# A fused attention and linear-attention block on one core: GpSimd's arithmetic moved to VectorE, and the gates' reciprocals rebuilt from log, exp and a Newton step

## The chip, the cores and the metric

The kernel runs on one core of a Trainium2 chip. The metric is the device time of one execution in microseconds: 2037.1 us, the median of three runs (2032.62 to 2038.48). The profile shows one more execution, which took 2037.28 us.

## The reference

One layer over 1024 tokens of width 2048, all in float32. A vector of shift, scale and gate is computed from `c` by a 2048 x 6144 product; the normalised input is modulated by it and projected by `w_in` (2048 x 7184). Group A has eight heads of differential attention, group B four heads of gated linear attention with a state carried from chunk to chunk of 64 tokens. Both outputs are normalised per head and multiplied by the SiLU of a projected gate. An output projection, a gated residual and a last RMSNorm end it. What matters here, in short:

```
proj = hn @ w_in                       # dq dk dv dg | gq gk gv gg glr
p    = softmax(mask(q k^T * scale))    # two maps per head
a    = p[:, 0] - lam * p[:, 1]
A    = rmsnorm(a @ v) * (1 - lam_init) * silu(dg)
B    = rmsnorm(gla(gq, gk, gv, log_sigmoid(glr @ w2 + b) / 16)) * silu(gg)
out  = rmsnorm(x + gate * (concat(A, B) @ w_out))
```

## The kernel before

Each matrix is held as two parts, a high one rounded to the type in which TensorE multiplies (fp32r) and a low one, the rest. A product takes three matmuls: high by high, high by low, low by high. So every weight piece goes through a small pipeline in `wload` (L169 to L186): SyncE loads 128 x 1024 numbers (512 KB) from memory into `wr` (two buffers), ScalarE casts them into the high half of `w` (L180, three buffers), and GpSimd subtracts that from the original into the low half (L181). TensorE then uses the piece in 24 matmuls of 512 columns, or 48 of 256. There are 298 pieces. For the 32 of the first stage the caller names VectorE in GpSimd's place (`first_a`, `first_b`).

The stages, in order of time: 0 to 200 us computes scale and shift from `wada` and accumulates the first projections beside it; then come eight units (two halves of 512 tokens by four groups), each with two attention heads (`attention`), projections and one linear-attention head (`gla`); from about 1600 us the output projection (L928 on). In attention, VectorE takes the row maxima from PSUM (L609), ScalarE the exponentials (L618), VectorE scales the second map by a column (L632) and adds the scaled first (L633), TensorE transposes, ScalarE and VectorE split the result (`split`, L229), and TensorE multiplies by the values (L660 to L662).

Beside the weights GpSimd does the second product of the rotary embedding (L520), three products of each head's normalisation (L566, L578, L580, but for the last head), and half of the 16 low parts of the second half's input (L906). It issues no DMA.

`silu_gate` (L238 to L245) makes a gate: ScalarE's exp(-x), one added on VectorE (L242), VectorE's reciprocal in two pieces of 256 columns (L244), and one product with the gate and a weight column (L245). There are 32 such gates of 128 x 512.

Two side jobs are fed through a staging tile of two buffers (`run_ahead`, L828): the second half's input is normalised row by row, and the residual gate is computed from `wgate`, four blocks of 16 rows, each row added on VectorE to `gacc` (L859). Their loads (L834) stand in the same SyncE queue as the weights' (L178).

The order on each engine is fixed when the program is built: the Tile framework simulates a timeline, takes priorities given in the code (weights are put 300 ahead, WSPAN), and writes one queue for each engine. An engine does its queue in that order; an instruction whose inputs are not there holds all behind it.

Of the kernel before, what the change touches and what calls it, by code (L numbers as in the profile page):

```python
# [10 lines left out]
F32 = mybir.dt.float32  # L11
F32R = mybir.dt.float32r
BF16 = mybir.dt.bfloat16
AF = mybir.ActivationFunctionType
# [5 lines left out]
P = 128  # L20
# [16 lines left out]
EVAC = 0  # L37
WSPAN = 300
FIN = 3
RCP = 256  # L40
PE_P = (4, 9, 14)
DVE0 = (1, 3, 5, 7, 9, 12)
DVE1 = (1, 3, 5, 7, 8, 9, 10, 12, 13, 14)
# [53 lines left out]
def body(ctx, tc, A, out):  # L97
# [71 lines left out]
    def wload(src, n, lo_eng=None, span=WSPAN, tile_=None):  # L169
        w_n[0] += 1  # L170
        with tc.high_priority(offset=span):
            raw = wr_p.tile([P, 1024], F32, name=f"wr{w_n[0]}", tag="wr")
            dst = raw[:, :n]
            if len(src.shape) == 3:
                dst = dst.rearrange("p (a b) -> p a b", a=src.shape[1])
            elif len(src.shape) == 4:
                dst = dst.rearrange("p (a b c) -> p a b c", a=src.shape[1], b=src.shape[2])
            nc.sync.dma_start(dst, src)  # L178
            w = tile_ if tile_ is not None else w_p.tile([P, 2, 1024], F32R, name=f"w{w_n[0]}", tag="w")
            paced = SC.copy(w[:, 0, :n], raw[:, :n])  # L180
            (lo_eng or G).tensor_tensor(w[:, 1, :n], raw[:, :n], w[:, 0, :n].bitcast(F32), ALU.subtract)  # L181
        for _ in range(pops(w_n[0])):
            if later:
                with tc.issue_after(paced.ins):
                    later.pop(0)()
        return w  # L186
# [42 lines left out]
    def split(hi, lo, src, lo_eng=None):  # L229
        SC.copy(hi, src)  # L230
        (lo_eng or V).tensor_tensor(lo, src, hi.bitcast(F32), ALU.subtract)  # L231
# [3 lines left out]
        nc.sync.dma_start(t, A["rope"][:, :, half * TOK:(half + 1) * TOK])  # L235
        return t

    def silu_gate(dst, src, wcol, tmp):  # L238
        SC.activation(tmp, src, AF.Exp, scale=-1.0)
        if dst is not src:  # L240
            SC.copy(dst, src)
        V.tensor_scalar_add(tmp, tmp, 1.0)  # L242
        for i in range(0, TOK, RCP):
            V.reciprocal(tmp[:, i:i + RCP], tmp[:, i:i + RCP])  # L244
        V.scalar_tensor_tensor(dst, dst, wcol, tmp, ALU.mult, ALU.mult)  # L245


    st_ctx = ExitStack()
# [231 lines left out]
    nc.sync.dma_start(ind, A["ind"])  # L480
    nc.sync.dma_start(dnw, A["dnw"])
    nc.sync.dma_start(gnw, A["gnw"])
    V.tensor_scalar_mul(dnw, dnw, 1.0 - LAM_INIT)
    ltri_f = misc.tile([P, 2, TOK], F32, name="ltri_f", tag="rt", bufs=2)
    nc.sync.dma_start(ltri_f[:, 0, :P], A["ltri"])
    V.tensor_copy(ltri, ltri_f[:, 0, :P])
# [25 lines left out]
    def rope(src, nm):  # L512
        rt = misc.tile([P, 2, TOK], F32, name=f"rt_{nm}", tag="rt", bufs=2)
        t1, sw = rt[:, 0, :], rt[:, 1, :]
        for m_ in range(2):
            for hh in range(2):
                o, i_ = m_ * 64 + hh * 32, m_ * 64 + (1 - hh) * 32
                SC.copy(sw[o:o + 32, :], src[i_:i_ + 32, :])  # L518
        V.tensor_mul(t1, src, rope_t[:, 0, :])
        G.tensor_tensor(sw, sw, rope_t[:, 1, :], ALU.mult)  # L520
        V.tensor_add(t1, t1, sw)
        return t1

# [59 lines left out]
    def attention(half, h, qt, kb, vb, g_t):  # L583
# [8 lines left out]
        for grp in range(2):  # L592
            at = []
            for b in (2 * grp, 2 * grp + 1):
# [34 lines left out]
                a_ = []  # L629
                for pi, (kk, n) in enumerate(pieces):  # L630
                    p0, p1 = pt[0, pi][:, :n], pt[1, pi][:, :n]
                    V.tensor_scalar(p1, p1, sm[:, 12:13], None, ALU.mult)  # L632
                    V.scalar_tensor_tensor(p0, p0, sm[:, 10:11], p1, ALU.mult, ALU.add)  # L633
                    a_.append(pt[0, pi])
                at.append(a_)
# [25 lines left out]
                    PE.matmul(dst, vh, aT[:, 1, sl], start=False, stop=False, skip_group_check=True)  # L661
                    PE.matmul(dst, vl, aT[:, 0, sl], start=False, stop=last and k == 1, skip_group_check=True)  # L662
            SC.copy(y[:, grp * 256:(grp + 1) * 256], av[:, :256])
        wf, wr2 = norm_stats([y], f"d{half}{h}", P, eps_l, V if (half, h) == (1, HEADS - 1) else G)
        V.scalar_tensor_tensor(g_t, wf[:, 0, :], sq_max, g_t, ALU.is_lt, ALU.mult)
        r_ = norm_finish(wf, eps_l, V if (half, h) == (1, HEADS - 1) else G)
        V.tensor_mul(y, y, r_)
        V.tensor_mul(y, y, g_t)
        mix_out(y, wr2, half, h)
# [90 lines left out]
    def unit(half, g, first, kdec):  # L760
# [4 lines left out]
        def gate_tile(i):  # L765
            s_ = src("dg", i)
            g_t = s_ if first else acc_p.tile([P, TOK], F32, name=f"g{half}_{i}", tag="g", bufs=2)
            tmp = misc.tile([P, 2, TOK], F32, name=f"gt{half}_{i}", tag="rt", bufs=2)
            silu_gate(g_t, s_, dnw, tmp[:, 0, :])
            return g_t  # L770

        def make_gq():
# [33 lines left out]
        for j in range(2):  # L806
            s_ = src("gg", 2 * g + j)
            tmp = misc.tile([P, 2, TOK], F32, name=f"ggt{half}{g}{j}", tag="rt", bufs=2)
            silu_gate(gg[:, j, :], s_, gnw[:, j:j + 1], tmp[:, 0, :])
        swap = half == 0 and g == GHEADS - 1  # L810
        if not first:
            pss = proj_a(A["wina"][A_AT[("gv", g)]], hn)
# [83 lines left out]
    def second_hn():  # L896
        while later:
            later.pop(0)()
        for k0 in range(0, KT, 2):
            tag = ("ka", "va", "kb")[k0 // 2 % 3]  # L900
            r3 = hd_p.tile([P, 2, TOK], F32, name=f"xtb{k0}", tag=tag, bufs=2 if tag == "kb" else None)
            nc.sync.dma_start(r3, hn_d[k0 // 2])
            for kk in range(2):
                kt = k0 + kk
                hn[kt] = hn_p.tile([P, 2, TOK], F32R, name=f"hn{kt}", tag=f"hn{kt}")
                split(hn[kt][:, 0, :], hn[kt][:, 1, :], r3[:, kk, :], lo_eng=V if kk else G)  # L906


    later += run_ahead(norm_rows())
# [137 lines left out]
```

## Time and profile before

| | |
|---|---|
| median of three runs | 2037.1 us |
| profiled execution | 2037.28 us, of which the span of instructions 2035.5 us |
| mean granted TensorE clock | 0.979 of full speed |
| TensorE matmuls busy | 1934.8 us, 95% |
| VectorE busy | 1364.1 us, 67% |
| ScalarE busy | 880.2 us, 43% |
| GpSimd busy | 762.8 us, 37% |

An engine is busy while an instruction of its own runs, also when this instruction stands still inside and waits for something that the profile does not show. The time outside the span (1.8 us) is not touched by the change. PEclk is the granted share of TensorE's clock in a stretch; 1.00 is 2.4 GHz, 0.5 is 1.2 GHz.

### The profile page before, as it was taken

What the parts mean: (1) busy time and instruction counts of PE and PEld (TensorE: products, weight loads), DVE (VectorE), ACT (ScalarE), POOL (GpSimd) and SP (SyncE); (2) the same over time, 40 slices, a digit from 0 to 9 for tenths busy, and PEclk for the clock granted to TensorE, in tenths of its full rate; (3) what the DMA queues carried; (4) which work ended last, traced back from release to release, by engine and by line L of the source; (5) the groups of instructions that cost most, each with busy time, mean ns of one, the idle gap of its engine ahead of it and who ended that gap; (6) DMA issues with size and microseconds to landing.
All of it is one profiled execution on the core that took longest, in us unless ns stands there. A gap on an engine that the chain in (4) does not pass through costs nothing.

```text
span 2035.5 us, 29315 instructions
## 1 busy us (share of the span) xinstructions
PE 1934.8 (95%) x11238; PEld 1695.4 (83%) x11238; DVE 1364.1 (67%) x2305; ACT 880.2 (43%) x1686; POOL 762.8 (37%) x357
## 2 busy tenths in 40 slices
PE   7999899999888999999998999899988999899998
PEld 5888888898778888889898888888876898688888
DVE  7998775577798658746675686667786664622234
ACT  4212655455433555544435544354444443422223
POOL 0000544424433446643443334353343334244442
PEclk9999999999999999999999999999998999899999
DMA  9874434332654343433343323433243642557443
GB/s 366 296 263 130 144 107 146 117 98 85 206 188 145 116 146 114 141 103 97 95 150 109 103 87 105 154 96 104 84 156 101 220 137 89 177 201 253 160 145 124
DMA packets 112192, 298.19 MB, mean 146 GB/s; under 512 B 11146, under 2 KB 32138, under 8 KB 111540
## 3 DMA queue, kind: packets, MB, share of 16 engines
q1 hardware_dynamic: 112052, 296.32, 44.2%
q8 instruction: 88, 1.44, 0.3%
q14 instruction: 52, 0.43, 0.1%
HBM read 258.00 MB, written 38.28 MB: 146 GB/s over the span
## 4 chain that ended last, share of the span: by engine, by line
PE 62%; DVE 20%; issue 6%; DMA 6%; ACT 4%; POOL 2%; SPq 0%; DVEq 0%; POOLq 0%; ACTq 0%
PE pa L219 5%; PE pa L220 5%; PE pa L221 5%; PE pa L990 4%; PE pa L991 4%; PE pa L992 4%; DMA stage<-in_wgate 2%; DVE gacc L859 2%; PE pb_dk L191 2%; PE pb_dk L193 2%; PE pb_dk L192 2%; PE pb_gg L191 2%; PE pb_gg L193 2%; PE pb_gg L192 2%; DVE p L632 1%
## 5 line engine op out<-in xcount | busy, mean ns | idle before, releaser
L181 POOL TENSOR_TENSOR w<-wr,w 128x1024 fp32r<-128x1024 f32 (+2 forms) x265 | 643.2, 2428 | 951.5 <-ACT w L180 883.6
L180 ACT CAST w<-wr 128x1024 fp32r<-128x1024 f32 (+2 forms) x297 | 304.3, 1025 | 439.1 <-PE pa L992 86.2
L219 PE MATMUL pa<-w,hn 128*128 128x256 f32 (+1 forms) x1152 | 330.9, 288 | 5.9 <-DVE gq L776 1.8
L221 PE MATMUL pa<-w,hn 128*128 128x256 f32 (+1 forms) x1152 | 332.0, 288 | 0.0
L220 PE MATMUL pa<-w,hn 128*128 128x256 f32 (+1 forms) x1152 | 331.8, 288 | 0.0
L219 PEld LDWEIGHTS pa<-w,hn 128*128 128x128 f32 x1152 | 223.6, 194 | 8.9 <-DVE gq L776 2.1
L221 PEld LDWEIGHTS pa<-w,hn 128*128 128x128 f32 x1152 | 223.8, 194 | 2.1 <-issue 0.7
L220 PEld LDWEIGHTS pa<-w,hn 128*128 128x128 f32 x1152 | 224.0, 194 | 1.8 <-issue 0.2
L618 ACT ACTIVATE p<-s,sm 128x512 f32<-128x512 f32 (+2 forms) x192 | 111.2, 583 | 207.3 <-DVE sm L615 113.5
L990 PE MATMUL pa<-w,mx 128*128 128x512 f32 x384 | 150.4, 393 | 0.3 <-DVE h L935 0.3
L991 PE MATMUL pa<-w,mx 128*128 128x512 f32 x384 | 150.4, 392 | 0.0
L992 PE MATMUL pa<-w,mx 128*128 128x512 f32 x384 | 149.7, 392 | 0.0
L609 DVE TENSOR_REDUCE sm<-s 128x1 f32<-128x512 f32 (+2 forms) x192 | 105.3, 550 | 49.8 <-PE s L606 47.4
L935 DVE TENSOR_TENSOR h<-pa,gbs 128x512 f32<-128x512 f32 (+1 forms) x24 | 14.9, 639 | 134.3 <-PE pa L992 120.6
L520 POOL TENSOR_TENSOR rt_k<-rt_k,rope 128x512 f32<-128x512 f32 x16 | 23.2, 1451 | 205.2 <-ACT rt_k L518 204.5
L231 DVE TENSOR_TENSOR aT<-tp,aT 128x512 fp32r<-128x512 f32 (+1 forms) x80 | 50.1, 626 | 72.4 <-ACT aT L230 72.3
L191 PE MATMUL pb_dg<-hn,w 128*128 128x512 f32 x224 | 89.2, 398 | 0.0
L193 PE MATMUL pb_dg<-hn,w 128*128 128x512 f32 x224 | 88.9, 397 | 0.0
L191 PE MATMUL pb_dk<-hn,w 128*128 128x512 f32 x224 | 88.9, 397 | 0.0
L192 PE MATMUL pb_dg<-hn,w 128*128 128x512 f32 x224 | 88.8, 396 | 0.0
L191 PE MATMUL pb_gg<-hn,w 128*128 128x512 f32 x224 | 88.7, 396 | 0.0
L193 PE MATMUL pb_dk<-hn,w 128*128 128x512 f32 x224 | 88.6, 395 | 0.0
(362 smaller groups left out, 4999.8 us busy)
## 6 DMA issues: line engine op xcount, KB each, us to landing
wr<-in_winb SPq DMA_DIRECT2D x142, 512.0 KB, 3.7
wr<-in_wina SPq DMA_DIRECT2D x72, 512.0 KB, 3.7
wr<-in_wout SPq DMA_DIRECT2D x64, 512.0 KB, 3.7
ada<-in_wada SPq DMA_DIRECT2D x44, 512.0 KB, 5.4
stage<-in_wgate SPq DMA_DIRECT2D x64, 256.0 KB, 2.6
mx<-mixd SPq DMA_DIRECT2D x32, 512.0 KB, 6.6
ada_kdec<-in_wada SPq DMA_DIRECT2D x20, 512.0 KB, 4.6
mixd<-wr_d SPq DMA_DIRECT2D x16, 512.0 KB, 3.1
```

The source lines that it names most:

```text
L180: paced = SC.copy(w[:, 0, :n], raw[:, :n])
L181: (lo_eng or G).tensor_tensor(w[:, 1, :n], raw[:, :n], w[:, 0, :n].bitcast(F32), ALU.subtract)
L191: PE.matmul(ps, w_hi, h[:, 0, :], start=first, stop=False)
L192: PE.matmul(ps, w_hi, h[:, 1, :], start=False, stop=False)
L193: PE.matmul(ps, w_lo, h[:, 0, :], start=False, stop=last)
L219: PE.matmul(o, ah, wh, start=st, stop=False, skip_group_check=True)
L220: PE.matmul(o, ah, wl, start=False, stop=False, skip_group_check=True)
L221: PE.matmul(o, al, wh, start=False, stop=kt == KT - 1, skip_group_check=True)
L618: SC.activation(p_[:, :n], pss[pi][:, :n], AF.Exp, bias=nm, scale=0.125, accum_out=sm[:, 4 + 2 * m_ + pi:5 + 2 * m_ + pi])
L990: PE.matmul(pss[t_], ah, wh, start=kt == 0, stop=False)
L991: PE.matmul(pss[t_], ah, wl, start=False, stop=False)
L992: PE.matmul(pss[t_], al, wh, start=False, stop=kt == KT - 1)
```

## The change

Four edits. All low parts, the rotary and the normalisation products that GpSimd made are now VectorE's. The second attention map is scaled on ScalarE (`SC.mul`) instead of VectorE. In `silu_gate` the reciprocal of d = 1 + exp(-x) becomes r = exp(-ln d) on ScalarE and one Newton step on VectorE (d r, then (d r - 2) r, whose sign is turned by a negated weight column, then the product with the gate). The constant RCP goes.

```diff
@@ wload
-            (lo_eng or G).tensor_tensor(w[:, 1, :n], raw[:, :n], w[:, 0, :n].bitcast(F32), ALU.subtract)
+            (lo_eng or V).tensor_tensor(w[:, 1, :n], raw[:, :n], w[:, 0, :n].bitcast(F32), ALU.subtract)
@@
-    def silu_gate(dst, src, wcol, tmp):
-        SC.activation(tmp, src, AF.Exp, scale=-1.0)
+    def silu_gate(dst, src, neg_w, tmp):
+
+        d, r_ = tmp[:, 0, :], tmp[:, 1, :]
+        SC.activation(d, src, AF.Exp, scale=-1.0)
         if dst is not src:
             SC.copy(dst, src)
-        V.tensor_scalar_add(tmp, tmp, 1.0)
-        for i in range(0, TOK, RCP):
-            V.reciprocal(tmp[:, i:i + RCP], tmp[:, i:i + RCP])
-        V.scalar_tensor_tensor(dst, dst, wcol, tmp, ALU.mult, ALU.mult)
+        V.tensor_scalar(d, d, 1.0, 1e37, ALU.add, ALU.min)
+        SC.activation(r_, d, AF.Ln)
+        SC.activation(r_, r_, AF.Exp, scale=-1.0)
+        V.tensor_mul(d, d, r_)
+        V.scalar_tensor_tensor(d, d, 2.0, r_, ALU.subtract, ALU.mult)
+        V.scalar_tensor_tensor(dst, dst, neg_w, d, ALU.mult, ALU.mult)
@@ rope
-        G.tensor_tensor(sw, sw, rope_t[:, 1, :], ALU.mult)
+        V.tensor_mul(sw, sw, rope_t[:, 1, :])
@@ attention
-                    V.tensor_scalar(p1, p1, sm[:, 12:13], None, ALU.mult)
+                    SC.mul(p1, p1, sm[:, 12:13])
@@
-        wf, wr2 = norm_stats([y], f"d{half}{h}", P, eps_l, V if (half, h) == (1, HEADS - 1) else G)
+        wf, wr2 = norm_stats([y], f"d{half}{h}", P, eps_l, V)
@@
-        r_ = norm_finish(wf, eps_l, V if (half, h) == (1, HEADS - 1) else G)
+        r_ = norm_finish(wf, eps_l, V)
@@ second_hn
-                split(hn[kt][:, 0, :], hn[kt][:, 1, :], r3[:, kk, :], lo_eng=V if kk else G)
+                split(hn[kt][:, 0, :], hn[kt][:, 1, :], r3[:, kk, :], lo_eng=V)
```

The scheduler lays all queues anew. VectorE's queue goes from 2159 rows to 2454, ScalarE's from 1271 to 1433, GpSimd's from 362 to 11.

Two places show what VectorE's queue gained and lost. The first is the start of the third block of gate rows, at 1256 us in the profile: `gacc` is the sum that a gate row is added to, `wf_d` a head's normalisation, `aT` the low part of a transposed map. Before:

```order
L577 SCALAR_TENSOR_TENSOR wf_d_10860<-wf_d_10860,vec 128x512
L859 SCALAR_TENSOR_TENSOR gacc_11386<-stage,vec,gacc_11386 128x512
L231 TENSOR_TENSOR aT_11191<-tp_11186,aT_11191 128x512
L859 SCALAR_TENSOR_TENSOR gacc_11386<-stage,vec,gacc_11386 128x512 x2
L579 TENSOR_SCALAR wf_d_10860<-wf_d_10860 128x512
L859 SCALAR_TENSOR_TENSOR gacc_11386<-stage,vec,gacc_11386 128x512
L667 TENSOR_TENSOR y_2_10611<-y_2_10611,wf_d_10860 128x512
```

And the same place after the change, with the line numbers of the changed kernel (L863 is the gate row, L180 the low part of a weight piece, L582 and L584 the two products that were GpSimd's L578 and L580, L247 a gate's Newton step):

```order
L581 SCALAR_TENSOR_TENSOR wf_d_10903<-wf_d_10903,vec 128x512
L863 SCALAR_TENSOR_TENSOR gacc_11431<-stage,vec,gacc_11431 128x512
L230 TENSOR_TENSOR aT_11236<-tp_11231,aT_11236 128x512
L247 SCALAR_TENSOR_TENSOR gt_4_12225<-gt_4_12225 128x512
L582 TENSOR_TENSOR wf_d_10903<-wf_d_10903 128x512
L863 SCALAR_TENSOR_TENSOR gacc_11431<-stage,vec,gacc_11431 128x512
L180 TENSOR_TENSOR w_12401<-wr_12399,w_12401 128x1024
L583 TENSOR_SCALAR wf_d_10903<-wf_d_10903 128x512
L863 SCALAR_TENSOR_TENSOR gacc_11431<-stage,vec,gacc_11431 128x512
L584 TENSOR_TENSOR wf_d_10903<-wf_d_10903 128x512
L863 SCALAR_TENSOR_TENSOR gacc_11431<-stage,vec,gacc_11431 128x512
L230 TENSOR_TENSOR aT_11250<-tp_11245,aT_11250 128x512
```

The weight piece and the two products now stand between the gate rows, and whatever one of them waits for, the rows behind it wait for too.

The second is one SiLU gate (`ggt`) on VectorE late in the second half. Before:

```order
L242 TENSOR_SCALAR ggt_13313<-ggt_13313 128x512
L755 TENSOR_TENSOR gg_11445<-to_11944,gg_11445 128x512
L609 TENSOR_REDUCE sm_12416<-s_12435 128x1
L755 TENSOR_TENSOR gg_11445<-to_11953,gg_11445 128x512
L244 RECIPROCAL ggt_13313<-ggt_13313 128x256 x2
L615 TENSOR_SCALAR sm_12416<-sm_12416 128x1
```

After, the same gate (L243, L246 and L247 are its add, its product d r and its Newton step):

```order
L180 TENSOR_TENSOR w_13449<-wr_13447,w_13449 128x1024
L243 TENSOR_SCALAR ggt_13366<-ggt_13366 128x512
L780 SCALAR_TENSOR_TENSOR gq_13301<-pb_gq_13237,gq_13301 128x512
L155 TENSOR_SCALAR sm_11980<-sm_11864 128x4
L613 TENSOR_REDUCE sm_12467<-s_12468 128x1
L613 TENSOR_REDUCE sm_12467<-s_12472 128x1
L246 TENSOR_TENSOR ggt_13366<-ggt_13366 128x512
L158 TENSOR_TENSOR sm_11980<-sm_11980,sm_11979 128x4
L619 TENSOR_SCALAR sm_12467<-sm_12467 128x1
L247 SCALAR_TENSOR_TENSOR ggt_13366<-ggt_13366 128x512
```

The two reciprocals are gone, and the scheduler put other work into the time that the gate now spends on ScalarE.

## Rows read from the trace of the kernel before

**Rows 1.** The page: busy time, share of the span, instructions of each engine.

```profile
PE 1934.8 (95%) x11238; PEld 1695.4 (83%) x11238; DVE 1364.1 (67%) x2305; ACT 880.2 (43%) x1686; POOL 762.8 (37%) x357
```

**Rows 2.** Stretches: length, busy us of PE, PEld, DVE, ACT, POOL, PEclk, DMA, GB/s.

```profile
0.00:200.00 200.00, 185.82 (x1036) 154.67 (x1037) 177.98 (x306) 57.53 (x82) 0.70 (x6) 0.97 0.77 266
...
500.00:700.00 200.00, 178.13 (x993) 153.46 (x993) 158.22 (x260) 86.53 (x168) 82.36 (x40) 0.96 0.50 162
700.00:1050.00 350.00, 346.75 (x2168) 311.98 (x2167) 235.27 (x397) 163.50 (x319) 166.59 (x81) 1.00 0.37 118
1050.00:1100.00 50.00, 44.84 (x216) 37.93 (x215) 34.62 (x36) 26.64 (x42) 20.66 (x10) 0.93 0.45 147
1100.00:1250.00 150.00, 149.24 (x901) 132.78 (x900) 101.82 (x180) 73.29 (x151) 56.22 (x25) 1.00 0.29 93
1250.00:1300.00 50.00, 42.77 (x246) 37.77 (x245) 44.85 (x65) 21.14 (x38) 19.60 (x10) 0.93 0.49 155
1300.00:1450.00 150.00, 148.49 (x852) 129.97 (x851) 98.92 (x157) 70.92 (x137) 66.83 (x30) 1.00 0.32 101
1450.00:1600.00 150.00, 134.67 (x721) 113.49 (x719) 109.72 (x173) 60.07 (x122) 54.36 (x26) 0.93 0.36 117
```

**Rows 3.** VectorE in order of time, third block of gate rows.

```profile
1256.90 2.78 DVE L577 SCALAR_TENSOR_TENSOR wf_d<-wf_d,vec 128x512 f32<-128x512 f32 x1
1259.61 0.74 DVE L859 SCALAR_TENSOR_TENSOR gacc<-stage,vec,gacc 128x512 f32<-128x512 f32 x1
...
1265.66 2.70 DVE L859 SCALAR_TENSOR_TENSOR gacc<-stage,vec,gacc 128x512 f32<-128x512 f32 x1 [1.58 <-DMA stage<-in_wgate]
1268.29 1.77 DVE L667 TENSOR_TENSOR y<-y,wf_d 128x512 f32<-128x512 f32 x1
```

**Rows 4.** GpSimd in order of time, the same stretch.

```profile
1256.50 2.64 POOL L181 TENSOR_TENSOR w<-wr,w 128x1024 fp32r<-128x1024 f32 x1 [4.76 <-issue]
...
1265.41 2.41 POOL L181 TENSOR_TENSOR w<-wr,w 128x1024 fp32r<-128x1024 f32 x1
```

**Rows 5.** SyncE's DMA issues in order of time, the same stretch.

```profile
1262.09 8.99 SPq L834 DMA_DIRECT2D stage<-in_wgate  x4
1271.13 0.42 SPq L178 DMA_DIRECT2D wr<-in_wina  x1
```

**Rows 6.** One source line each: duration in ns, shortest/median/longest.

```profile
L859 DVE SCALAR_TENSOR_TENSOR gacc<-stage,vec,gacc x60: 651/752/2976, 600.9 to 1522.8; 128x512 f32<-128x512 f32 x60
L628 DVE TENSOR_TENSOR sm<-sm,vec x64: 141/151/156, 238.0 to 1703.8; 128x1 f32<-128x1 f32 x64
L632 DVE TENSOR_SCALAR p<-p,sm x96: 268/478/2675, 238.8 to 1704.3; 128x512 f32<-128x512 f32 x48, 128x128 f32<-128x128 f32 x16, 128x256 f32<-128x256 f32 x16, 128x384 f32<-128x384 f32 x16
```

**Rows 7.** Groups by line and shape: count, busy us, mean ns, idle before.

```profile
L859 DVE SCALAR_TENSOR_TENSOR gacc<-stage,vec,gacc 128x512 f32<-128x512 f32 x60 | 73.5, 1225 | 20.8 <-DMA stage<-in_wgate 20.2
L244 DVE RECIPROCAL gt<-gt 128x256 f32<-128x256 f32 x32 | 54.0, 1723 | 0.3
L633 DVE SCALAR_TENSOR_TENSOR p<-p,sm,p 128x512 f32<-128x512 f32 x48 | 48.5, 1022 | 0.1
L231 DVE TENSOR_TENSOR aT<-tp,aT 128x512 fp32r<-128x512 f32 x48 | 32.8, 683 | 49.6 <-ACT aT L230 49.5
L181 DVE TENSOR_TENSOR w<-wr,w 128x1024 fp32r<-128x1024 f32 x24 | 29.2, 1219 | 2.6 <-ACT w L180 2.6
L632 DVE TENSOR_SCALAR p<-p,sm 128x512 f32<-128x512 f32 x48 | 27.9, 595 | 0.0
L627 DVE TENSOR_TENSOR sm<-sm,vec 128x1 f32<-128x1 f32 x64 | 24.7, 386 | 1.6
L181 POOL TENSOR_TENSOR w<-wr,w 128x1024 fp32r<-128x1024 f32 x253 | 621.5, 2458 | 918.8 <-ACT w L180 851.0 <-issue 39.4 <-DMA wr<-in_winb 11.5
L571 ACT ACTIVATE wf_d<-wf_d,vec 128x512 f32<-128x512 f32 x16 | 11.6, 727 | 23.3 <-DVE wf_d L570 23.3
L942 ACT ACTIVATE h<-h,otot 128x512 f32<-128x512 f32 x16 | 10.9, 715 | 1.6 <-DVE otot L162 1.6
```

More of the change, by code (lines that the diff above doesn't have):

```diff
@@ L39 @@
 FIN = 3
-RCP = 256
 PE_P = (4, 9, 14)
@@ L482, in body @@
     nc.sync.dma_start(gnw, A["gnw"])
-    V.tensor_scalar_mul(dnw, dnw, 1.0 - LAM_INIT)
+    V.tensor_scalar_mul(dnw, dnw, LAM_INIT - 1.0)
+    V.tensor_scalar_mul(gnw, gnw, -1.0)
     ltri_f = misc.tile([P, 2, TOK], F32, name="ltri_f", tag="rt", bufs=2)
@@ L768, in gate_tile @@
             tmp = misc.tile([P, 2, TOK], F32, name=f"gt{half}_{i}", tag="rt", bufs=2)
-            silu_gate(g_t, s_, dnw, tmp[:, 0, :])
+            silu_gate(g_t, s_, dnw, tmp)
             return g_t
@@ L808, in unit @@
             tmp = misc.tile([P, 2, TOK], F32, name=f"ggt{half}{g}{j}", tag="rt", bufs=2)
-            silu_gate(gg[:, j, :], s_, gnw[:, j:j + 1], tmp[:, 0, :])
+            silu_gate(gg[:, j, :], s_, gnw[:, j:j + 1], tmp)
         swap = half == 0 and g == GHEADS - 1
```

## The prediction

> **What bounds the kernel now.** I read the page first, then the table by stretches, then VectorE, GpSimd and SyncE in order of time where that table is worst, then the groups by line. The reader is to see three things.
>
> First, TensorE is the engine that the span follows: 1934.8 of 2035.5 us busy [rows 1]. What can be won is its idle time, 100.7 us, and what the lower clock takes after it paused. The idle time is not spread evenly. From 700 to 1050 us TensorE is idle 3.3 of 350 us at a granted clock of 1.00, and 1100 to 1250 and 1300 to 1450 us look alike (0.8 and 1.5 us): 650 us with 5.5 us idle. Four thin stretches stand against that: 500 to 700, 1050 to 1100, 1250 to 1300 and 1450 to 1600 us. There 450 us have 21.9 + 5.2 + 7.2 + 15.3 = 49.6 us idle, and the granted clock is 0.96, 0.93, 0.93 and 0.93, which at most costs 8.0 + 3.5 + 3.5 + 10.5 = 25.5 us. Together 75 us [rows 2].
>
> Second, VectorE is the fuller engine exactly there: 347 of 450 us in the thin stretches, 77%, against 436 of 650 us, 67%, in the full ones; GpSimd does not follow this pattern (39% and 45%) [rows 2]. The first 200 us have a full VectorE, but GpSimd works only 0.7 us in them; the change does not reach them.
>
> Third, part of VectorE's fullness is standing still. At 1256.90 us a 512-wide instruction took 2.78 us and ended 0.54 us after GpSimd's weight piece of 1256.50 to 1259.14; at 1265.66 us a gate row took 2.70 us and ended 0.54 us after the piece of 1265.41 to 1267.82 [rows 3, 4]. The same gate row takes 0.74 us right between them, and its median over 60 is 0.752 us with a longest of 2.976 [rows 3, 6]. So an instruction of VectorE that reads two operands from SBUF waits inside itself until GpSimd is done; one that reads PSUM does not show it (the transposed maps' low part: 683 ns as a mean [rows 7]).
>
> Why that stops TensorE is in SyncE's queue: four gate rows' loads hold it from 1262.09 for 8.99 us, because a staging buffer comes free only when VectorE has added its row, and the next weight load is issued at 1271.13 [rows 5].
>
> **The change, part by part.** The profiled execution took 2037.28 us, its span 2035.5; the median of the runs, 2037.1, is the same to 0.2 us, so I sum against 2037.
>
> Low parts of the weights: 266 pieces leave GpSimd. VectorE makes a 128x1024 one in 1.219 us, in the first stage where GpSimd rests; GpSimd takes 2.458 us [rows 7]. 254 x 1.22 = 310 us, and the twelve narrower ones at most 1 us each: 321 us in all on VectorE.
>
> The other products that move: 32 rotary, 45 of the normalisation, 8 low parts of the second input, each 128x512; at 0.69 us (the 683 ns of the same width) 59 us.
>
> Gates: 64 reciprocals at 1.72 us go, 110 us (the second group of 32 is like the one shown); 32 products at 0.69 and 32 Newton steps at 0.75 come, 46 us. The add and the last product stay. ScalarE gains 64 instructions of at most 0.727 us, 47 us [rows 7]. The gate's own chain barely changes: 3.44 us of reciprocals become 0.73 + 0.73 + 0.69 + 0.75 = 2.9 us and two changes of engine. I cost it at nothing either way.
>
> Second map: 96 instructions at about 0.6 us leave VectorE, 57 us, and cost ScalarE at most 0.715 each, 69 us [rows 7]. ScalarE goes from 880 to 880 + 47 + 69 = 996 us, 49% of the span; it is then still the emptier one, which is the cover. Without it the price is the difference, 96 x (0.715 - 0.478) = 23 us [rows 6, 7].
>
> The Trainium skill, "ScalarE: Activation LUTs", section "Rules for kernel authors", speaks against this edit: plain products belong on VectorE, not on ScalarE. The rows agree on one instruction (715 ns against a median of 478); by that rule, with none of it hidden, the sum below would come out 23 us higher, at 2023. I weigh it little, since TensorE waits where VectorE is full.
>
> VectorE so far: 1364 - 110 - 57 + 321 + 59 + 46 = 1623 us. From this comes off what it stood still for GpSimd. Three groups show it: gate rows 60 x (1225 - 752) = 28 us, second map's addition 48 x (1022 - 752) = 13 us, a one-column product 64 x (386 - 151) = 15 us, its twin one row on being the 151 [rows 6, 7]: 56 of 147 us, 38%. What is left of VectorE's time after the first 200 us, without these three and without what is removed, is 1364 - 178 - 147 - 167 = 872 us. It loses between nothing (all like the PSUM readers) and 38%, 331 us; I take 20%, 174 us, since about half of its instructions read PSUM or one operand. So VectorE ends at 1623 - 56 - 174 = 1393 us, 68%, about as now, with ends of 1236 and 1567 us (61% and 77%).
>
> The gain is therefore not a lighter VectorE but an evener one: the new 1.22 us pieces come one in about 7 us (1835 us after the first stage by 266), also in the full stretches, while the holds of 2 us go where VectorE is behind. In the 13 us of rows 3 three instructions stood still for 2.0 + 1.9 + 1.1 = 5.0 us, 39% of the time. New in such 13 us are two pieces and two products, 2 x 1.22 + 2 x 0.69 = 3.8 us, but as work that is done while the loads of the gate rows are under way.
>
> Thin stretches: between nothing, if the added pieces take the place of the holds, and all 75 us, if the stretches become like the full ones. I take half, nearest to the 39%: -37 us.
>
> Full stretches: after its cast a weight piece took GpSimd 2.46 us; now it takes 1.22 us and what VectorE has ahead of it. And the change adds a wait: behind a low part that waits for its cast stands all that VectorE does, row maxima, splits and gate rows, and TensorE waits for each of them. Between a gain of 5.5 us (the idle time there) and one piece's time for each, a loss of 266 x 1.22 = 325 us. I take 0, near the lower end: a piece that finds one such instruction ahead of it (1.22 + 1.22 us) is ready when GpSimd's was.
>
> Start and end: no change in the first 200 us. The last piece is 1.2 us shorter; within the range. Sum: 2037 - 37 = 2000 us.
>
> **The rivals.** *VectorE's queue stops TensorE (slower).* One queue now holds the weights and all of attention. For it: VectorE at up to 77%, in a fixed order, with each low part waiting for a cast that itself waits for TensorE. Against it: a piece is 1.2 us shorter, and in the full stretches VectorE is idle a third of the time. Place: the 650 us of full stretches and those like them. Price: each late piece 1.2 us; one in six, 44, makes +53, with the forecast's gain 2053. It decides from 37 / 1.2 = 31 late pieces. The Trainium skill, "Perfetto Trace Analysis", section "Optimizing Scalar/DVE Operations", supports a part of it: a saturated VectorE is a reason to give work to ScalarE or even GpSimd, which is the reverse of this change; but it adds that those two share a read port, so that such a move might not help. The fullest stretch after the first, 1250 to 1300 us, has VectorE busy 44.9 of 50 us, part of it standing still.
>
> *The side loads set the thin stretches.* If the gate rows wait for their loads and not for VectorE, only a few us come back: one hold of about 1.8 us in each of four stretches, -7, 2030. Against it: the 60 rows waited 20.8 us for loads and stood still 28 [rows 7].
>
> *All of it goes.* With no holds, the lower clock that follows a pause goes too: -75, 1962. For it: what separates thin from full stretches is VectorE's share alone.
>
> *The change doesn't do what it says:* VectorE would stand still for something other than GpSimd, and 1623 us of work, 80%, would wait as before. Rows 3 and 4 leave 2 in 100 for that; it would be slower.
>
> **How the numbers follow.** Chances: forecast 0.45 (own range 1980 to 2020), all goes 0.20, side loads 0.13, VectorE's queue 0.18, no effect as said 0.02, and 0.02 for gain and loss that cancel. A measurement of this kernel can tell 0.3%, 6 us, from no change. Faster by more: 0.45 + 0.20 + half of 0.13, 0.72; within: the other half, the 0.02 and a little of the slower cases, 0.10; slower: 0.18. The range leaves out 1 in 10 on each side: 1960, beyond the case in which all goes, and 2045, where about half of the slower case lies beyond.
>
> **What would show it.** Right: VectorE's gate rows all near 0.75 us and the second map's additions near 0.75; low parts at 1.22; VectorE near 1390 us busy, ScalarE near 1000; TensorE's idle time in the stretches around the gate rows halved, with fewer drops of its clock; idle time in the full stretches as before. Wrong: TensorE idle before projection matmuls with a VectorE low part as the releaser, spread over the full stretches; or gate rows at 0.75 us and the thin stretches unchanged, their weights still late on SyncE.

## The result and the profile after

The changed kernel takes 1971.4 us as the median of 4 runs (1967.8 to 1972.3), against 2035.8 of the kernel before beside it: a ratio of 0.9685 [0.9672, 0.9698], 64 us less. The forecast was 2000 with a range of 1960 to 2045: the direction and the range hold, the size is too small.

The page after, as [rows 1]: busy time, share of the span, instructions.

```profile
PE 1914.2 (97%) x11238; PEld 1682.8 (85%) x11238; DVE 1336.2 (68%) x2561; ACT 968.9 (49%) x1846; POOL 0.7 (0%) x6
```

The span fell by 65.4 us, from 2035.5 to 1970.1. TensorE's idle time fell from 100.7 to 55.9, which is 44.8 of it. The other 20.6 us are busy time of the same 11238 instructions. The mean granted clock rose from 0.979 to 0.985; by these two means some 12 us go with the clock (an estimate: 1914.2 x 0.985 / 0.979 = 1926), and the rest was not followed. VectorE got 256 instructions more and is busy 28 us less.

The stretches after, with the columns of [rows 2]:

```profile
200.00:500.00 300.00, 298.18 (x1904) 271.39 (x1903) 211.59 (x435) 192.50 (x376) 0.00 (x0) 1.00 0.40 123
500.00:700.00 200.00, 192.02 (x1094) 166.51 (x1094) 154.82 (x331) 106.05 (x211) 0.00 (x0) 0.98 0.57 179
700.00:1050.00 350.00, 350.00 (x2133) 313.54 (x2132) 238.63 (x443) 190.57 (x359) 0.00 (x0) 1.00 0.40 124
1050.00:1100.00 50.00, 49.56 (x336) 45.62 (x335) 28.99 (x45) 27.69 (x50) 0.00 (x0) 1.00 0.28 85
1250.00:1300.00 50.00, 50.00 (x259) 42.46 (x258) 33.17 (x57) 26.66 (x44) 0.00 (x0) 1.00 0.49 147
1450.00:1600.00 150.00, 143.73 (x919) 128.75 (x918) 100.68 (x206) 81.92 (x166) 0.00 (x0) 0.98 0.52 175
1650.00:1720.00 70.00, 57.41 (x263) 46.28 (x262) 39.43 (x76) 25.79 (x62) 0.00 (x0) 0.85 0.46 152
```

The full stretch stayed full, 500 to 700 us lost most of its pauses, and 1250 to 1300 has none left. The stretch 200 to 500, which the prediction did not list, went from 287.54 to 298.18 us busy. From 1650 to 1720 there are now 12.6 us idle at a clock of 0.85. That pause is not new: it stands before the 9863rd to the 9887th of TensorE's 11238 matmuls, and in the kernel before the 9866th to the 9884th waited from 1746 to 1758 us. It grew from 7.8 to 12.6 us. The stretch 200 to 500 and the one with that pause in the kernel before:

```profile
200.00:500.00 300.00, 287.54 (x1780) 258.63 (x1779) 213.29 (x379) 170.25 (x338) 132.13 (x65) 0.99 0.38 118
```

```profile
1720.00:1790.00 70.00, 62.25 (x279) 49.89 (x278) 34.27 (x68) 25.58 (x63) 22.62 (x9) 0.90 0.46 154
```

Since the kernel runs ahead of its old times, two VectorE lines serve as landmarks: the row maxima of attention and the gate rows. Each row gives count, shortest/median/longest ns, and first and last start. Before:

```profile
L609 DVE TENSOR_REDUCE sm<-s x192: 226/590/694, 226.5 to 1699.2; 128x1 f32<-128x512 f32 x96, 128x1 f32<-128x128 f32 x32, 128x1 f32<-128x256 f32 x32, 128x1 f32<-128x384 f32 x32
```

After:

```profile
L613 DVE TENSOR_REDUCE sm<-s x192: 218/590/694, 223.7 to 1635.6; 128x1 f32<-128x512 f32 x96, 128x1 f32<-128x128 f32 x32, 128x1 f32<-128x256 f32 x32, 128x1 f32<-128x384 f32 x32
L863 DVE SCALAR_TENSOR_TENSOR gacc<-stage,vec,gacc x60: 665/746/753, 594.0 to 1465.7; 128x512 f32<-128x512 f32 x60
```

The gate rows began at 600.9 and ended at 1522.8 [rows 6]. So 2.8 us come before the first row maximum, 4.1 more up to the first gate row, 50.2 between the first and the last gate row, 6.5 up to the last row maximum, and 1.8 in the output stage. The longest gate row fell from 2976 to 753 ns.

The queues were laid anew, so a landmark is not quite the same amount of work. A count of TensorE's matmuls in the two traces is a second measure (how many have started at a time of the kernel before, and how much earlier the next one starts after the change):

| matmuls started | time before, us | earlier after, us |
|---|---|---|
| 2814 | 500 | 13.6 |
| 3805 | 700 | 32.2 |
| 5971 | 1050 | 37.3 |
| 6185 | 1100 | 44.8 |
| 7084 | 1250 | 44.1 |
| 7328 | 1300 | 56.2 |
| 8178 | 1450 | 50.1 |
| 8897 | 1600 | 68.8 |
| 11238 (end) | 2035 | 65.4 |

By this count the four thin stretches became 18.6 + 7.5 + 12.1 + 18.7 = 57 us shorter, the three full ones 2 us longer; 14 us come before 500 us, and 3 are lost from 1600 on.

Groups after, as [rows 7]:

```profile
L180 DVE TENSOR_TENSOR w<-wr,w 128x1024 fp32r<-128x1024 f32 x277 | 338.2, 1221 | 290.6 <-ACT w L179 289.4
L863 DVE SCALAR_TENSOR_TENSOR gacc<-stage,vec,gacc 128x512 f32<-128x512 f32 x60 | 44.5, 742 | 13.0 <-DMA stage<-in_wgate 12.6
L637 DVE SCALAR_TENSOR_TENSOR p<-p,sm,p 128x512 f32<-128x512 f32 x48 | 35.3, 744 | 6.5 <-ACT p L636 6.5
L631 DVE TENSOR_TENSOR sm<-sm,vec 128x1 f32<-128x1 f32 x64 | 10.0, 156 | 1.4
L636 ACT ACTIVATE p<-p,sm 128x512 f32<-128x512 f32 x48 | 33.9, 722 | 12.8 <-DVE sm L632 12.7
```

All three groups that stood still are at their undisturbed durations: 1225 to 742, 1022 to 744 and 386 to 156 ns. Instructions that read one operand had stood still as well, here one of the normalisation before and after; the addition in the gates (L242) fell from 1283 and 1437 to 418 and 417 ns:

```profile
L579 DVE TENSOR_SCALAR wf_d<-wf_d 128x512 f32<-128x512 f32 x16 | 18.7, 1171 | 5.5 <-POOL wf_d L578 5.5
```

```profile
L583 DVE TENSOR_SCALAR wf_d<-wf_d 128x512 f32<-128x512 f32 x16 | 6.7, 416 | 0.1
```

What TensorE waited for: us in total, times, longest. Three rows of the list before:

```profile
PE av L661 <- DVE aT L231: 12.7, 5, 5.4
PE tp L648 <- DVE p L633: 8.0, 7, 2.9
PE o L743 <- DVE sr L231: 5.8, 5, 2.7
```

The rows that answer to the first and the third in the list after, and VectorE's own longest wait (there is no row for the addition to `p` any more):

```profile
PE av L665 <- DVE aT L230: 1.0, 2, 0.8
PE o L747 <- DVE sr L230: 0.9, 1, 0.9
...
DVE w L180 <- ACT w L179: 297.2, 160, 5.8
```

Summed over the whole list, TensorE waited 62 us in 45 waits for VectorE before and 28 us in 22 after; for ScalarE 29 and 16; for DMA 0.2 and 3. These differences, 34 + 14 - 3 = 45 us, are its whole gain in idle time. No row of either list names a weight piece.

The chain of work that ended last, followed back from the end, by engine. Before:

```profile
PE 62%; DVE 20%; issue 6%; DMA 6%; ACT 4%; POOL 2%; SPq 0%; DVEq 0%; POOLq 0%; ACTq 0%
```

After:

```profile
PE 86%; DMA 6%; DVE 5%; ACT 1%; issue 1%; DVEq 0%; ACTq 0%
```

### The profile page after: what moved, and what is told of

Same layout as the page of the kernel before. It is cut to its first block, busy times and chain, and to the rows that moved or that the text cites. A ratio compares the mean times of both kernels' runs of the same rounds, so it can differ in the third digit from the quotient of the medians.

```text
span 1970.1 us, 29377 instructions
## 1 busy us (share of the span) xinstructions
PE 1914.2 (97%) x11238; PEld 1682.8 (85%) x11238; DVE 1336.2 (68%) x2561; ACT 968.9 (49%) x1846; POOL 0.7 (0%) x6
## 4 chain that ended last, share of the span: by engine, by line
PE 86%; DMA 6%; DVE 5%; ACT 1%; issue 1%; DVEq 0%; ACTq 0%
PE pa L218 8%; PE pa L220 8%; PE pa L219 8%; PE pa L994 4%; PE pa L995 4%; PE pa L996 4%; PE pb_dq L191 2%; PE pb_dk L190 2%; PE pb_dk L191 2%; PE pb_dq L192 2%; PE pb_dq L190 2%; PE pb_dk L192 2%; PE pb_gg L190 2%; PE pb_gg L191 2%; PE pb_dg L190 2%; PE pb_gg L192 2%
## 5 line engine op out<-in xcount | busy, mean ns | idle before, releaser
L180 DVE TENSOR_TENSOR w<-wr,w 128x1024 fp32r<-128x1024 f32 (+2 forms) x297 | 352.5, 1187 | 300.2 <-ACT w L179 297.2
L218 PEld LDWEIGHTS pa<-w,hn 128*128 128x128 f32 x1152 | 220.0, 191 | 4.9 <-DVE gq L780 1.9
L219 PEld LDWEIGHTS pa<-w,hn 128*128 128x128 f32 x1152 | 220.4, 191 | 2.0 <-issue 0.2
L220 PEld LDWEIGHTS pa<-w,hn 128*128 128x128 f32 x1152 | 220.3, 191 | 1.5 <-issue 0.5
L190 PE MATMUL pb_gg<-hn,w 128*128 128x512 f32 x224 | 89.3, 398 | 2.1 <-ACT g L242 2.1
L192 PE MATMUL pb_gg<-hn,w 128*128 128x512 f32 x224 | 88.8, 396 | 0.0
L191 PE MATMUL pb_gg<-hn,w 128*128 128x512 f32 x224 | 88.7, 396 | 0.0
L191 PE MATMUL pb_dk<-hn,w 128*128 128x512 f32 x224 | 88.4, 395 | 0.0
L190 PE MATMUL pb_dq<-hn,w 128*128 128x512 f32 x224 | 88.2, 394 | 0.0
L191 PE MATMUL pb_dg<-hn,w 128*128 128x512 f32 x224 | 88.1, 393 | 0.0
L192 PE MATMUL pb_dq<-hn,w 128*128 128x512 f32 x224 | 88.0, 393 | 0.0
L191 PE MATMUL pb_dq<-hn,w 128*128 128x512 f32 x224 | 87.8, 392 | 0.0
L190 PE MATMUL pb_dg<-hn,w 128*128 128x512 f32 x224 | 87.8, 392 | 0.0
```

Source lines behind the costliest of these rows:

```text
L180: (lo_eng or V).tensor_tensor(w[:, 1, :n], raw[:, :n], w[:, 0, :n].bitcast(F32), ALU.subtract)
L190: PE.matmul(ps, w_hi, h[:, 0, :], start=first, stop=False)
L191: PE.matmul(ps, w_hi, h[:, 1, :], start=False, stop=False)
L192: PE.matmul(ps, w_lo, h[:, 0, :], start=False, stop=last)
L218: PE.matmul(o, ah, wh, start=st, stop=False, skip_group_check=True)
L219: PE.matmul(o, ah, wl, start=False, stop=False, skip_group_check=True)
```

## The experiments

The theory: VectorE stands still inside its instructions while GpSimd makes a low part, and TensorE waits for the small results behind them. The rivals: VectorE simply had too much work (then the lighter gates and the map make the gain); GpSimd's results came late, and the gain is that nobody waits for them any more; VectorE's queue is a new bound; the side loads set the time. Times are medians, each ratio against the kernel before on the same chip.

**GpSimd works, and nobody reads what it makes.** The changed kernel, and behind each weight piece one GpSimd product of 768 columns into a scratch that nobody reads. The queues of the other four engines are the same.

```diff
+    junk = const.tile([P, 768], BF16, name="junk")
...
             (lo_eng or V).tensor_tensor(w[:, 1, :n], raw[:, :n], w[:, 0, :n].bitcast(F32), ALU.subtract)
+            if lo_eng is None and n >= 768:
+                G.tensor_tensor(junk, w[:, 0, :768].bitcast(F32), w[:, 0, :768].bitcast(F32), ALU.subtract)
```

> The changed kernel, with one GpSimd subtraction per weight piece put back that nobody uses: it reads 768 columns of the piece's high part twice from SBUF and writes a scratch tile; no instruction waits for it, and the queues of the other four engines stand exactly as in the changed kernel. Theory (VectorE stands still inside an instruction while GpSimd reads SBUF): 264 such products of about 1.8 us make some 475 us of GpSimd, against 763 in the kernel before, so about 0.6 of what the change took away comes back: gate rows with a mean near 1.0 us and a longest over 2 us, VectorE 100 to 150 us busier, TensorE's pauses back around the gate rows, time 2000 to 2015 us. Rival (the gain came from GpSimd's slow results no longer being waited for): nobody waits here, so 1971 us within 6, gate rows at 0.75.

2002.6 us, 0.9844 [0.9829, 0.9859]: 31 of the 64 us are lost again. Its page:

```profile
PE 1931.2 (96%) x11238; PEld 1691.8 (84%) x11238; DVE 1503.1 (75%) x2561; ACT 964.2 (48%) x1846; POOL 561.3 (28%) x270
```

The same 2561 VectorE instructions take 167 us more. GpSimd and then VectorE in order of time show how:

```profile
1253.58 1.47 POOL L183 TENSOR_TENSOR junk<-w 128x768 bf16<-128x768 f32 x1 [5.49 <-ACT w L180]
1260.49 1.47 POOL L183 TENSOR_TENSOR junk<-w 128x768 bf16<-128x768 f32 x1 [5.44 <-ACT w L180]
```

```profile
1253.71 1.89 DVE L250 SCALAR_TENSOR_TENSOR gt<-gt 128x512 f32<-128x512 f32 x1
...
1260.83 1.68 DVE L674 TENSOR_TENSOR y<-y,wf_d 128x512 f32<-128x512 f32 x1
```

Both end 0.55 us after GpSimd's instruction (1255.60 against 1255.05, 1262.51 against 1261.96), as the two in [rows 3, 4] did by 0.54. TensorE waits 38 us for VectorE here, against 28. The gate rows' mean was 881 ns, where 1.0 us had been expected. So GpSimd's work alone makes VectorE stand still and costs 31 us, though no data passes from GpSimd to anybody.

One thing does wait for GpSimd here, against what had been expected: a buffer of `w` comes free only when GpSimd has read it, and ScalarE's casts waited for that. The row, and the chain that ended last in this run:

```profile
ACT w L180 <- POOL junk L183: 20.5, 11, 2.6
```

```profile
PE 66%; DVE 18%; DMA 7%; issue 5%; ACT 4%; POOL 0%; DVEq 0%; ACTq 0%; POOLq 0%; SPq 0%
```

GpSimd has 0% of that chain, and VectorE's share goes from 5% back to 18%, near the 20% of the kernel before. Of TensorE's waits those for VectorE grew by 10.5 us against the changed kernel, those for ScalarE by 4.1. So the standing still carries most of the loss; no run has it without the wait for the buffer.

The Trainium skill, "SBUF — State Buffer", section "SBUF: two separate sides", states the rule: VectorE and GpSimd share a pair of ports, an exclusive lock. Whichever starts first, a GpSimd instruction or one of VectorE with two inputs from SBUF or in a two-port mode, has the pair for its whole instruction, and the other blocks fully. The rows agree, both ways: VectorE stands still as shown, and GpSimd's product takes 1.47 us in the 12 cases in which VectorE was idle at its start, but 2.42 as a mean in the 151 in which VectorE was making a low part.

**The same products in three pieces, and copies.** Three products of 256 columns in place of the one of 768; and one copy of 768 columns, which reads one operand. The other queues are the same in both.

```diff
-                G.tensor_tensor(junk, w[:, 0, :768].bitcast(F32), w[:, 0, :768].bitcast(F32), ALU.subtract)
+                for q in range(0, 768, 256): G.tensor_tensor(junk[:, q:q + 256], ...)
```

```diff
-                G.tensor_tensor(junk, w[:, 0, :768].bitcast(F32), w[:, 0, :768].bitcast(F32), ALU.subtract)
+                G.tensor_copy(junk, w[:, 0, :768].bitcast(F32))
```

> As the kernel after the change, with the idle GpSimd product of 768 columns behind each weight piece cut into three of 256 columns that read and write the same numbers; nothing is left out of the result, and the queues of the other four engines are those of the run with one product of 768. Question: does the time lost there (2002.6 against 1971.4 us) come from the sum of what VectorE stands still (167 us) or from the length of one hold (up to 1.2 us on a gate row)? If from the sum: VectorE again near 1500 us busy and the time 1995 to 2005. If from the length: the longest gate row near 1.1 us instead of 1.95, VectorE still well above 1336, and the time 1971 to 1980, as with the single-operand copies (66 us, 1972.2). Three short products have a larger total on GpSimd if each has a fixed part, which works against the second case.

> As the run with GpSimd subtractions that nobody uses, but each is a copy: one operand of 768 columns read from SBUF, the same scratch tile written. Queues of the other engines as in the changed kernel. Theory (VectorE stands still whenever GpSimd works on SBUF): the loss goes with GpSimd's busy time; if a copy takes about half of a subtraction (1 us, 264 us in all), half of the 31 us, 1980 to 1992 us, and gate rows' longest over 1.2 us. Rival (only GpSimd's two-operand instructions hold VectorE): 1971 us within 6, gate rows at 0.75.

Three pieces: 1987.1 us, 0.9759 [0.9743, 0.9775]. Copies: 1972.2 us, 0.9691 [0.9677, 0.9706], no loss. Page and gate rows, first with three pieces:

```profile
PE 1919.0 (97%) x11238; PEld 1683.8 (85%) x11238; DVE 1435.9 (72%) x2561; ACT 966.6 (49%) x1846; POOL 767.1 (39%) x798
...
L866 DVE SCALAR_TENSOR_TENSOR gacc<-stage,vec,gacc x60: 661/750/1184, 597.7 to 1484.8; 128x512 f32<-128x512 f32 x60
```

Then with copies:

```profile
PE 1914.8 (97%) x11238; PEld 1682.9 (85%) x11238; DVE 1401.8 (71%) x2561; ACT 967.4 (49%) x1846; POOL 411.6 (21%) x270
...
L866 DVE SCALAR_TENSOR_TENSOR gacc<-stage,vec,gacc x60: 664/750/1311, 591.7 to 1467.9; 128x512 f32<-128x512 f32 x60
```

Neither expectation on the three pieces came true: 1987 lies between. With much the same longest gate row (1184 and 1311 ns) one costs 16 us and the other 1, so the length of a hold does not decide alone. The sum orders the runs: 66 us of standing still cost 1 us, 100 cost 16, 167 cost 31. With so few points this is an order, not a law, and ScalarE's waits for a free buffer (3.1, 17.7 and 20.5 us) give the same one. For the copies both expectations missed: VectorE is held, and it costs nothing. GpSimd's busy time does not order them at all (412, 767 and 561 us).

**The parts of the change.** In the kernel before, only the low parts of the weights on VectorE:

```diff
-            (lo_eng or G).tensor_tensor(w[:, 1, :n], raw[:, :n], w[:, 0, :n].bitcast(F32), ALU.subtract)
+            (lo_eng or V).tensor_tensor(w[:, 1, :n], raw[:, :n], w[:, 0, :n].bitcast(F32), ALU.subtract)
```

> The kernel before with one edit: the low parts of the weights on VectorE. GpSimd keeps its rotary and normalisation products and half of the second input's low parts (about 115 us). VectorE has the reciprocals and the second map still. Theory: most of GpSimd's time and so of VectorE's standing still is gone, VectorE near 1500 us busy, 1985 to 2005 us. Rival (VectorE's queue, heavier by 321 us): 2036 us or more.

1996.7 us, 0.9813 [0.9798, 0.9827]. VectorE's busy time rises by 54 us, where 136 had been expected, and the kernel gains 38.

```profile
PE 1930.2 (97%) x11238; PEld 1691.3 (85%) x11238; DVE 1418.5 (71%) x2571; ACT 884.3 (44%) x1686; POOL 120.1 (6%) x91
```

Everything off GpSimd, but gates and map as before (the changed kernel with these two edits undone):

```diff
-                    SC.mul(p1, p1, sm[:, 12:13])
+                    V.tensor_scalar(p1, p1, sm[:, 12:13], None, ALU.mult)
...
-        V.tensor_scalar(d, d, 1.0, 1e37, ALU.add, ALU.min)
...
+        for i in range(0, TOK, RCP):
+            V.reciprocal(tmp[:, i:i + RCP], tmp[:, i:i + RCP])
```

> The changed kernel with the old gates (reciprocals on VectorE) and the second map scaled on VectorE again; GpSimd still does no arithmetic. VectorE gets about 110 - 46 + 45 = 110 us more than the changed kernel's 1336, some 1445 us. Theory (standing still for GpSimd was the cost): most of the 64 us stay, 1978 to 1995 us. Rival (VectorE's load was the cost, and the two relieving edits pay): 2020 us or more. Second rival (VectorE's queue stops TensorE once it is this full): above 2036.

1982.5 us, 0.9744 [0.9724, 0.9764]: 14 us more come from the last 120 us of GpSimd's work. VectorE is busy 1427 us, 91 more than after, and 52 of the 64 us are there. These 14 us need not all be holds: in the kernel before VectorE waited 12.7 us and ScalarE 15.6 us for results of GpSimd's rotary and normalisation products, and the runs do not separate the two. The longest of these waits in total:

```profile
ACT wr_d L230 <- POOL wf_d L566: 11.0, 6, 3.0
```


The reverse, gates and map changed in the kernel before, with GpSimd's work left where it was (the diff of these two edits is above):

> The kernel before with the two relieving edits alone (gates by log, exp and Newton; second map scaled on ScalarE); GpSimd keeps all its work. VectorE loses about 110 us of work but still stands still for GpSimd. Theory: a small part of the gain, 2015 to 2030 us, gate rows still with a mean near 1.2 us. Rival (load): 1975 to 1995 us.

2033.5 us, 0.9992 [0.9982, 1.0002]: nothing, less than expected.

```profile
PE 1929.7 (95%) x11238; PEld 1690.0 (83%) x11238; DVE 1261.7 (62%) x2210; ACT 964.3 (47%) x1846; POOL 758.1 (37%) x357
...
L864 DVE SCALAR_TENSOR_TENSOR gacc<-stage,vec,gacc 128x512 f32<-128x512 f32 x60 | 66.7, 1111 | 17.8 <-DMA stage<-in_wgate 17.3
```

VectorE has 102 us less to do, the gate rows still take 1111 ns, and TensorE waits 63 us for VectorE as before. ScalarE has 84 us more to do, but TensorE's waits for it went from 29 to 24 us, so it hides no gain. VectorE's amount of work is not what cost the time.

Only the gates back to reciprocals, in the changed kernel:

```diff
-        V.tensor_scalar(d, d, 1.0, 1e37, ALU.add, ALU.min)
...
+            V.reciprocal(tmp[:, i:i + RCP], tmp[:, i:i + RCP])
```

> The changed kernel with the old gates alone (two reciprocals of 256 columns on VectorE); the second map stays on ScalarE. VectorE gets 110 - 46 = 64 us more. Both relieving edits together are worth 11 us without GpSimd (1982 against 1971). Theory (a long VectorE instruction, 1.72 us, delays what TensorE waits for; the map's products are short): most of it is the gates, 1978 to 1984 us. Rival (it is the second map): 1968 to 1974 us.

1981.5 us, 0.9728 [0.9708, 0.9748]. So 10 of the last 11 us are the gates'; the 1 us left for the map is within the spread of the runs.

**VectorE's queue.** If low parts on VectorE are often late, one buffer of cast weights less must hurt.

```diff
-    w_p = ctx.enter_context(tc.tile_pool(name="w", bufs=3))
+    w_p = ctx.enter_context(tc.tile_pool(name="w", bufs=2))
```

> The changed kernel with two buffers for the weight pieces instead of three. This asks why VectorE's queue, in which the low parts wait for their casts, does not stop TensorE. Theory: a piece is made while TensorE works on the two before it, so a late low part finds cover; with two buffers the cover is one piece of about 5.4 us less cast, low part and queue. Then TensorE pauses before many pieces: 298 pieces at 0.3 to 1 us, 2060 to 2270 us. Rival (VectorE is simply never late): 1971 to 1990 us.

1990.1 us, 0.9779 [0.9759, 0.9798]: 19 us more, far below the 2060 or more expected of late low parts and at the edge of the rival's range. Most of it is not even theirs: TensorE's 1037th matmul, at 200 us in the kernel before, starts 12.3 us later than in the changed kernel, and up to there VectorE made the low parts before the change, too. With two buffers the list of TensorE's waits names a low part of a weight for 6.9 us in 6 waits; with three, for none.

**The side loads.** Four staging buffers in place of two for the second half's input, and the early load of the output stage (`xse`) into buffers that are free sooner; first in the changed kernel, then in the kernel before.

```diff
+            if wide and "s2" not in side:
+                side["s2"] = hd_p.tile([P, 2, TOK], F32, name="stage2", tag="va")
...
-    later += run_ahead(norm_rows())
+    later += run_ahead(norm_rows(), wide=True)
...
-    xs_early = [hd_p.tile([P, 4, 256], F32, name=f"xse{n}", tag="vb", bufs=3) for n in range(2)]
+    xs_early = [hd_p.tile([P, 4, 256], F32, name=f"xse{n}", tag=("stage", "kb")[n], bufs=(None, 2)[n]) for n in range(2)]
```

> The changed kernel with two edits of buffers: while the second half's input is normalised, four staging buffers instead of two (the second pair in a tile that the first half leaves unused), and the two early loads of the residual's input go to buffers that come free sooner. What is left of TensorE's pauses in the changed kernel stands at 556 to 600 us, in the chain of store, load and two VectorE instructions of a staging buffer (10 us with the lower clock), and at 1670 to 1700 us behind those early loads (20 us). Theory (SyncE's queue and the staging buffers set these two): both go, 1945 to 1962 us. Rival (VectorE sets them too): 1966 to 1976 us.

> The kernel before with the two edits of buffers alone (four staging buffers while the second half's input is normalised, early residual loads into buffers that come free sooner); GpSimd keeps its work. Asks whether the pauses of the kernel before could have been cured at SyncE's staging without freeing VectorE. Theory (both add up: the holds of VectorE and the staging buffers are two causes): about what it brings in the changed kernel, 15 us, 2012 to 2026 us. Rival (the holds reach TensorE only by way of the staging loads): most of the 64 us, 1970 to 1995 us.

In the changed kernel 1955.9 us, 0.9611 [0.9587, 0.9635], 15 us better; in the kernel before 2036.2 us, 1.0006 [0.9994, 1.0017], nothing, where 10 us or more had been expected either way. The gate rows keep their two staging buffers in both. The two stretches, in the changed kernel with the buffers:

```profile
550.00:600.00 50.00, 47.06 (x297) 41.43 (x296) 42.41 (x102) 24.41 (x52) 0.00 (x0) 1.00 0.74 242
1650.00:1720.00 70.00, 62.79 (x280) 50.47 (x279) 37.27 (x64) 22.82 (x46) 0.00 (x0) 0.93 0.45 146
```

Without them the second has 57.41 us at 0.85, and the first this row:

```profile
550.00:600.00 50.00, 43.91 (x226) 36.78 (x225) 36.08 (x90) 22.90 (x49) 0.00 (x0) 0.93 0.66 203
```

On top of the freed buffers, the map back on VectorE, and in another kernel the gate rows spread out in the second half:

```diff
-                    SC.mul(p1, p1, sm[:, 12:13])
+                    V.tensor_scalar(p1, p1, sm[:, 12:13], None, ALU.mult)
```

```diff
-    pops = lambda n: n % 3 != 0
+    pops = lambda n: n * 4 % 7 < 4
```

> The run with the side loads freed (1956 us), with the second map scaled on VectorE again. Without GpSimd both relieving edits were worth 11 us and the gates 10, which leaves about 1 for the map. Theory: within 6 us of 1956. Rival (products belong on VectorE, which takes 0.48 us against ScalarE's 0.72 and saves two changes of engine): 1940 to 1949 us.

> The run with the side loads freed (1956 us), with the gate rows of the second half handed out with four of seven weight pieces instead of two of three. What is left of TensorE's pauses there stands at 1450 to 1500 us, in the last block of gate rows (12 us with the lower clock). Theory (the rows are dealt out in bursts, and a burst holds SyncE's queue): 1946 to 1954 us. Rival (the scheduler puts the rows where it wants, so the number does nothing): 1956 within 6.

The map on VectorE: 1962.2 us, 0.9638 [0.9619, 0.9657], 6 us more, which is not clear of the spread (1951.9 to 1959.9 us without it, 1957.8 to 1963.0 with it). Gate rows spread out: 1948.8 us, 0.9576 [0.9557, 0.9595], the best version here, 23 us below the changed kernel; all four of its runs lie below all four without it. That it works by way of SyncE's queue was not shown.

## Why the prediction was right in kind and too small

*VectorE stands still for GpSimd, and that is the gain.* Right, shown with identical queues on four engines. The three groups came out at the durations that the prediction took for undisturbed.

*VectorE's sum, 1393 us.* It ended at 1336, inside the two ends of 1236 and 1567. The standing still, taken as 56 + 174 = 230 us, is 1623 - 1336 = 287 by the same sum. The 20% left out the instructions that read one operand, and those stood still too: the addition in the gates and the normalisation's L579 alone account for 42 us (16.3 + 13.8 + 12.1). ScalarE ended at 969 against 996; low parts take 1.221 us against 1.22.

*Thin stretches, half of 75 us.* This is the mis-sized term: about 57 us by the count of matmuls, where -37 had been put. The measured time also lies below the 1980 to 2020 us that the forecast had for itself. *Everything else at 0* is the second: about 14 us come from before 500 us. The list of thin and full stretches left out 200 to 500 us, where 12.5 us of idle time became 1.8, with no gate row in it: the holds act wherever GpSimd has a piece to do. *Full stretches at 0* was right, about 2 us. "All of it goes", -75, was nearer than the forecast; what it lacks is the pauses that stayed, at 550 to 600 and 1450 to 1600 us.

*"Why that stops TensorE is in SyncE's queue."* Wrong in the path. Of TensorE's waits from 1250 to 1300 us the list before has one row, and it names no weight:

```profile
PE av L661 <- DVE aT L231: 7.2, 2, 5.4
```

ScalarE had made its half of that transposed map at 1265.10 (0.58 us from 1264.52); VectorE made the other at 1271.85, behind the two held instructions of [rows 3]:

```profile
1264.52 0.58 ACT L230 CAST aT<-tp 128x512 fp32r<-128x512 f32 x1
```

```profile
1271.85 0.68 DVE L231 TENSOR_TENSOR aT<-tp,aT 128x512 fp32r<-128x512 f32 x1
```

The two stood still 2.0 and 1.1 us, more than the 1.82 us that TensorE waited for this half. The other wait, 5.41 us, ended in the same way: ScalarE had made its half at 1274.34, and VectorE had two more held instructions before its own:

```profile
1274.38 2.88 DVE L859 SCALAR_TENSOR_TENSOR gacc<-stage,vec,gacc 128x512 f32<-128x512 f32 x1
...
1277.97 2.33 DVE L627 TENSOR_TENSOR sm<-sm,vec 128x1 f32<-128x1 f32 x1
...
1284.10 0.54 DVE L231 TENSOR_TENSOR aT<-tp,aT 128x384 fp32r<-128x384 f32 x1
```

So VectorE's queue did stop TensorE, in the kernel before: by low parts of activations that stood behind held instructions. The gate rows' loads are part of that chain too: VectorE waited 0.93 us for one at 1262.99 and 1.58 us for the next at 1265.66, which SyncE had issued at 1262.09 [rows 5], just after the row before had ended (1262.06). How much of the delay goes over the staging was not measured: the run with more staging (1.0006) widens it for the second input's rows alone.

*Gates, cost nothing either way.* Right while GpSimd works, as far as the run with both edits shows it (relief alone: 0.9992), wrong without it: 10 us. Whether the reciprocals' length or the 60 us more of VectorE's work does it was not separated.

*The map's 23 us at most are covered by ScalarE.* Right: the map on ScalarE is 1 us better in one pair and 6 in the other, both within the spread, and in neither is it worse. An instruction takes ScalarE 722 ns, against VectorE's median of 478 [rows 6]. The rule of the Trainium skill ("ScalarE: Activation LUTs", "Rules for kernel authors") that plain products belong on VectorE agrees with these two numbers, but no pair of runs gets faster by it.

*Rival "VectorE's queue stops TensorE".* Fell. VectorE stood 297 us at the head of its queue for casts, and TensorE's waits name no low part of a weight; even two buffers cost 19 us, not a slower kernel than before. How much of the 28 us that TensorE still waits for VectorE stands behind such a low part was not measured. *Rival "side loads set the thin stretches".* Fell as the first cause: the gate rows had two staging buffers in every run, and 1050 to 1100 and 1250 to 1300 us became full all the same. But the side loads are a good part of what is left: the chain after the change passes at 550 to 600 us through the staging of the second input, and at 1670 us through `xse`, which holds SyncE (start, us):

```profile
1670.90 8.83 SPq L925 DMA_DIRECT2D xse<-in_x  x2
```

Freeing both gave 15 us; the two were not tried one by one. Why the pause at 1650 to 1720 us is 4.8 us longer than it was before the change was not followed further than these loads.

## What to carry to other kernels

An engine that nobody seems to wait for can cost time by holding another one inside its instructions: compare the shortest, median and longest duration of one line before calling an engine busy, and test it with idle work on the suspected engine while all other queues stay the same. Read what a pause waits for from the list of waits, and not from the nearest long row in another queue. When one kernel runs ahead of the other, compare the same work (the n-th matmul) and not the same times. Relief (a lighter engine, more buffers) can be worth nothing while the hold is there and 10 to 15 us once it is gone, so each should be tried again after the main cause is removed.

## What the runs showed that I had not expected

- Holds can be free: copies on GpSimd made VectorE stand still 66 us and cost 1 us.
- GpSimd is held as well: its copy takes 0.83 us undisturbed, 1.56 as a mean, and 1.80 when it starts while VectorE makes a low part.
- Cutting GpSimd's product in three made GpSimd busier (561 to 767 us), and yet VectorE stood still less (167 to 100 us).
- 102 us less work on VectorE, at 62% of the span, changed nothing that can be measured.
